# A second buffer for the output weights' pieces, and the mean of the last 256 tokens subtracted by adding DMAs

## The chip, the cores and the metric

The kernel runs on one core of a Trainium2 chip. The core has a matrix engine (TensorE, PE in the profile), a vector engine (VectorE, DVE), a scalar engine (ScalarE, ACT), a general engine (GpSimd, POOL) and SyncE (SP), which here only issues DMAs. They run side by side, each through its own list of instructions in order, and wait for each other by semaphores; DMAs run on 16 engines of their own. The metric is the time of one execution on the device in microseconds.

## The reference

One decoder layer over 1024 tokens of width 2048, all in float32:

```python
h = x @ w_in + b_in
q, k, v, g_attn, u_pool, g_pool = split(h)
a = banded_sink_attention(q, k, v, sinks, bias, valid) * silu(g_attn)   # 16 heads, window 128
b = multiscale_pool(u_pool, w_pool, pool_scale) * silu(g_pool)          # windows 2, 4, 8, 16
mix = concat([a, b]) @ w_out
ple = sigmoid(x @ w_gate_ple) * (p @ w_ple)
y = layer_norm(2 ** 0.25 * x + mix + ple, ln_gain, ln_bias)
```

The layer norm subtracts from every token the mean over its 2048 channels, divides by the standard deviation, and applies a gain and a bias for each channel.

## The kernel before

**Layout and precision.** Everything is kept with channels on the 128 partitions and tokens along the free axis. Every float32 operand is split into a high part (rounded, by ScalarE's cast) and a low part (the rest, by VectorE's subtraction), and each product is three matmuls: high by high, low by high, high by low (`mm3`, L181 to L185).

**Products.** A job multiplies two blocks of 128 output channels by half of the input channels for all 1024 tokens. Of the four quarter products of its 2 by 2 block form, seven combined ones are enough (a fast matrix product; their names are p1 to p7, their operands b11, b21, t1 and so on). One of these products is 12 matmuls of 128 x 512, about 2.7 us, and is called a tick: a counter of the program, `clock`, is raised by one after each, and all side work is booked by it. `after(n, fn)` records fn at the n-th tick from now; `later(n, fn)` does so as well, and puts what fn records behind the marked newest instructions of the engines. The final order on each engine is made by the scheduler of the language from that, with the data dependencies; the order of a queue is fixed before the run.

**Weights.** Weight pieces arrive in the tiles raw (512 KB each, five buffers), are split into wh (ScalarE, L816) and wl (VectorE, L126), four units ahead of TensorE.

**Stages.** s1 and s2: queries, keys, values and the other inputs, one half of the input channels after the other; s3: the rest with the per-layer embedding; s4 and s5: the output projection of the pooled and of the attended half; s6: the last 256 tokens of the output projection. Tokens 0 to 767 go through s5 with 384 columns a matmul, tokens 768 to 1023 through s6 (`run_plain`) with plain products of 256 columns.

**Attention beside s2.** For each pair of heads and quarter of the tokens, `heads` books by ticks: loads of the queries (s<-q) and of two bias masks (s<-in_rel), a split, score products (sc, L613), maxima on VectorE (L616), exponentials on ScalarE (L632), transposes (tr, L649), and value products (pv, L665). Their tiles are slots, of which 15 are handed round in turn.

**Centred output weights, beside s2.** `centre_weights` reads the attended half of w_out in 32 pieces of 256 KB through one tile, cw, sums their rows on VectorE (wsum, L950), and then reads all 32 again, subtracts the mean over the output channels (cw, L126) and stores them (wc). So the attended half of the projection has mean zero over the channels and needs no mean subtracted later. A piece is loaded at its tick and used two ticks later; the next is loaded at that same tick.

**The rest of the mean.** s4 leaves its sums (embedding, residual and pooled half) in DRAM (co, 16 blocks of 1024 tokens) and adds them up over the channel blocks in csum. `split_total` and `mean_to_subtract` turn csum into minus the mean of each token (L992). For tokens 0 to 767 it is taken away in s5: for four of the output blocks by adding csum on VectorE (d<-d,csum), for the others by one more matmul at the end of a product, with a constant matrix w64 and the split mean z (`less_mean`, L1007). For the last 256 tokens each of the 16 output blocks gets one such matmul in `run_plain` (L515). In s5 a finished block gets what lies in co added by a DMA of POOL (d<-co or part<-co, L436) and is squared for the norm six ticks later.

**The end.** `norm_scale` and `norm_out` scale tokens 0 to 767 while s6 runs; the last 256 tokens are scaled after it.

Of the kernel before, what the change touches and what calls it, by code (L numbers as in the profile page):

```python
# [24 lines left out]
F32 = mybir.dt.float32  # L25
F32R = mybir.dt.float32r
AF = mybir.ActivationFunctionType
ALU = mybir.AluOpType
# [3 lines left out]
P = 128  # L32
T = 512
H = 4 * P
D = 2048
NB = 16
# [14 lines left out]
F1, F2 = 768, 256  # L51
# [14 lines left out]
class Layer:  # L66
# [203 lines left out]
    def two(self):  # L270
        return self.tile(self.twos, [P, 2, self.F], "two")
# [227 lines left out]
    def run_plain(self, g):  # L499

        nc = self.nc
        (job,), order = self.groups[g]
        for i in range(2):
            ps = self.bank(BANKS[0][i], 2)[:, :F2]
            final = job.mean and i
            for u in range(2):
                wh, wl = self.take()
                for k in range(4):
                    f = slice(k * P, (k + 1) * P)
                    mm = self.mm3(ps, (wh[:, f], wl[:, f]), self.x_plain(4 * u + k), u + k == 0, False)  # L510
                if final and not u:
                    t = self.new_part(job.b[i])
                    nc.tensor.matmul(ps, self.ident, t, start=False, stop=False, skip_group_check=True)
                if u:
                    mm = self.less_mean(ps, F1)  # L515
                self.mark("PE", mm)
                self.feed_raw()
                if u and final:
                    job.done(job.b[i], ps)
                    nc.vector.tensor_copy(out=t, in_=ps)  # L520
                elif u:
                    t = self.new_part(job.b[i])
                    self.add_to(t, ps, False)
                    job.done(job.b[i], t)
                self.tick()
# [49 lines left out]
    def heads(self, h, j, half):  # L575

        nc, g = self.nc, j // 4
# [5 lines left out]
        two = lambda t: t.rearrange("p (j t) -> p j t", j=2)  # L583

        def begin():
            f = slice(h * T + 256 * half, h * T + 256 * half + 256)
            q = self.slot()[:, :T]
            rq.append(q)
            for i in range(2):
                self.load(two(q)[:, i], self.qd[j + i][:, f])  # L590
            for i in range(2):
                bias.append(self.slot()[:, :T].rearrange("p (e k) -> p e k", e=2))
                self.load(bias[i], self.rel[j + i])
# [82 lines left out]
                    self.load(self.pre[j + i][:, f], pre[0][:, i])  # L676

        begin()
        self.later(3, split)
        for n in range(2):  # L680
            for i in range(2):
                self.after(6 + 4 * n, lambda n=n, i=i: score(n, i))
            self.after(9 + 4 * n, lambda n=n: shift(n))
            self.after(15 + 4 * n, lambda n=n: trans(n))
            for i in range(2):
                self.after(10 + 4 * n, lambda n=n, i=i: softmax(n, i))
                self.later(12 + 4 * n, lambda n=n, i=i: share(n, i))
            self.after(21 + 4 * n, lambda n=n: value(n))


    def gate_ahead(self, j):
# [245 lines left out]
    def centre_weights(self, at, by):  # L937

        nc = self.nc
        cells = [(b, h) for b in range(NB) for h in range(2)]  # L940
        sums = self.fix.tile([P, 8, NB], F32, name="wsum")
        mean = self.fix.tile([P, 8], F32, name="wmean")
        now = []

        def fetch(b, h):
            now.append(self.load(self.tile(self.cw, [P, H], "cw"), self.wout[b, 0][:, h * H : h * H + H]))

        def add_up(b, h):
            k = now.pop().rearrange("p (k m) -> p k m", k=4)
            nc.vector.reduce_sum(sums[:, 4 * h : 4 * h + 4, b : b + 1], k, axis=mybir.AxisListType.X)  # L950

        def take_mean():
            nc.vector.reduce_sum(mean.rearrange("p (k b) -> p k b", b=1), sums, axis=mybir.AxisListType.X)
            nc.vector.tensor_scalar(out=mean, in0=mean, scalar1=1.0 / D, scalar2=None, op0=ALU.mult)

        def centre(b, h):
            w = now.pop()
            k = w.rearrange("p (k m) -> p k m", k=4)
            m = mean[:, 4 * h : 4 * h + 4].rearrange("p (k m) -> p k m", m=1).broadcast_to([P, 4, P])
            self.tt(k, k, m, ALU.subtract)  # L960
            self.load(self.wc[b, 0][:, h * H : h * H + H], w)

        for step in (add_up, centre):
            for c in cells:
                self.after(at, lambda c=c: fetch(*c))
                self.later(at + 2, lambda c=c, step=step: step(*c))
                at += by if step is centre and c[0] % 3 else 2
            if step is add_up:
                self.later(at + 1, take_mean)
                at += 2  # L970

    def split_total(self, total, w, cut):
# [9 lines left out]
    def mean_to_subtract(self, total, w):  # L982

        nc = self.nc
        h = F1 // 2
        for f, pieces in self.total_parts:
            ps = self.bank("sc", 2)
            for i, t in enumerate(pieces):  # L990
                nc.tensor.matmul(ps, w, t, start=i == 0, stop=i == 1)
            nc.scalar.activation(total[:, f], ps, AF.Copy, scale=-64.0 / D)  # L992
        step = self.one["new"]("q")[:, :h]
        self.tt(step, total[:, h:F1], total[:, :h], ALU.subtract)
        self.z, self.w64, self.total = {}, w, total
        a, b = slice(0, 64), slice(64, P)
        zs = [self.tile(self.twos, [P, 2, h], "two", F32R).rearrange("p h t -> p (h t)") for _ in range(2)]
        hi = self.one["new"]("hi")
        for at, src in ((0, total[:, :h]), (h, step), (F1, total[:, F1:])):
            n = src.shape[-1]  # L1000
            z = self.z[at] = zs[at // F1][:, at % F1 : at % F1 + n]
            nc.scalar.copy(out=hi[b, :n], in_=src[b])
            nc.scalar.copy(out=z[a], in_=src[a])
            self.tt(z[b], src[b], hi[b, :n].bitcast(F32), ALU.subtract)
# [18 lines left out]
    def norm_sums(self, sums, a, first, last):  # L1023

        for b in range(a.shape[-1] // P):
            self.nc.tensor.matmul(sums[:, b : b + 1], a[:, b * P : (b + 1) * P], self.ones[:, 0:1], start=first and b == 0, stop=last,
                                  skip_group_check=True)

    def norm_scale(self, L, wait=0):
# [55 lines left out]
    def run(self):  # L1085
        nc, tc, fix = self.nc, self.tc, self.fix
# [18 lines left out]
        co = [self.scratch("co") for _ in range(NB)]  # L1105
# [14 lines left out]
        ga, gp, u = ([(win, *p) for p in pairs(b, 4)] for b in (GA0, GP0, U0))  # L1120
# [63 lines left out]
        for o in reversed(BESIDE):  # L1184
            u = UNITS[o]
            operand[u] = ExitStack()
            self.xp[u] = self.pool(f"x_{u}", 1, operand[u], reuse_waits="tile")
        parts, work, over = ExitStack(), ExitStack(), ExitStack()
# [76 lines left out]
        self.turn.clear()  # L1265
        self.ident = fix.tile([P, P], F32, name="ident")
        make_identity(nc, self.ident)
        self.ones = fix.tile([P, P], F32, name="ones")
        nc.gpsimd.memset(self.ones, 1.0)
        self.mhalf = fix.tile([P, 8], F32, name="mhalf")  # L1270
        nc.gpsimd.memset(self.mhalf, -0.5)
# [10 lines left out]
        work = ExitStack()  # L1282
        self.new_part = lambda b: self.tile(pp, [P, 2, T], "part")
        self.slot_n = T
        self.slots = self.work_pool("slots0", 15, work)
        self.kv = self.work_pool("kv", 1, over)

        def build_kv(b, build, group, halves=(0, 1)):
# [5 lines left out]
        t = 9  # L1294
# [18 lines left out]
        for i in range(n3):  # L1313
            if i == 1:
                over.close()
                work.close()
                work, over = ExitStack(), ExitStack()
# [6 lines left out]
            if i == n3 - 2:  # L1324

                over.close()
                work.close()
                work = ExitStack()
                self.slot_n = T
                six[:] = 5 * [pp] + 3 * [self.work_pool("p8", 3, work)]  # L1330
                self.slots = self.work_pool("slots1", 8, work)
                self.twos = self.work_pool("twos1", 4, work)
                self.new_part = part_of_six
                for n, b in enumerate(s3[-4].b + s3[-3].b):
                    self.after((1, 1, 5, 6)[n], lambda b=b: self.gate_ahead(b - GA0))
                pooled()
                for n, step in enumerate(make_pooled):
                    self.after((10, 13, 16, 19, 22, 28, 31)[n], step)
                for n, b in enumerate(b for j in s3[-2:] for b in j.b):
                    self.after(16 + 2 * n, lambda b=b: self.gate_ahead(b - GA0))  # L1340
            first = self.groups[g + i][0][0]
# [8 lines left out]
        csum = []  # L1350
# [54 lines left out]
        w64 = self.tile(d0, [P, P], "w64", F32R, bufs=1)  # L1405
        self.later(9, lambda: self.split_total(csum[0], w64, [(0, T), (T, 2 * T)]))
        self.later(10, lambda: self.mean_to_subtract(csum[0], w64))
        self.new_part = new_d
        one = self.one = self.norm_begin(F1, 0, lambda kind: self.tile(lns, [P, F1], "sq" if kind == "sq" else "q", F32R if kind == "hi" else F32,
                                                                       bufs=1 if kind == "sq" else 2))  # L1410
# [119 lines left out]
```

## Time and profile before

Three runs took 1445.77, 1445.88 and 1448.65 us; the median is 1445.88. The profiled execution took 1448.33 us, of which the span from the first to the last instruction is 1446.6.

| Engine | busy us | share of the span | instructions |
|---|---|---|---|
| TensorE, matmuls | 1429.2 | 99% | 6820 |
| VectorE | 1115.5 | 77% | 2045 |
| ScalarE | 792.1 | 55% | 1565 |
| GpSimd | 232.8 | 16% | 339 |

The mean granted clock of TensorE was 0.996 of full speed. Matmuls overlap in the profile, so TensorE's busy time says that it is not idle, not that it runs at its peak; its gaps are in the list of waits. A line of a timeline has start, duration, engine, line, operation and tiles (written <- read), and in brackets the idle time of the engine before it and what ended it. SPq stands for SyncE's queue of DMA issues. A line of a list of waits has the total, the number of waits and the longest, all in us. The stages in time: s1 to about 180 us, s2 with the attention to about 700, s3 to 1108, s4 to 1260, s5 to 1383, s6 to 1430, then the last norm.

### The profile page before, as it was taken

The page shows a single profiled execution, that of the slowest core. Times are in us where ns is not written, and L with a number is a line of the kernel's source. Part 1 is how long each engine was busy: PE and PEld are TensorE (multiplying, and loading weights), DVE is VectorE, ACT ScalarE, POOL GpSimd, SP SyncE. Part 2 cuts the span into 40 slices and gives each one's busy share as a digit, 9 for nine tenths or more (in the row PEclk, how much of TensorE's full clock was granted, in tenths as well). Part 3 has the DMA queues.
Part 4 walks back from the last instruction along what each step waited for, and adds up shares of the span by engine and source line. Part 5 has one row for each costly group of instructions (what it writes and reads, how often), then busy time and mean ns, then how long its engine had stood idle before and what let it go on. Part 6 is the DMA issues. An engine that isn't in the chain of part 4 may idle for free.

```text
span 1446.6 us, 20400 instructions
## 1 busy us (share of the span) xinstructions
PE 1429.2 (99%) x6820; PEld 1210.5 (84%) x6820; DVE 1115.5 (77%) x2045; ACT 792.1 (55%) x1565; POOL 232.8 (16%) x339
## 2 busy tenths in 40 slices
PE   9999999999999999999999999999999999999996
PEld 7888887888888888888888888888888888899996
DVE  6859567787788877878768876867678665987787
ACT  6546375665667656665664444443356433654476
POOL 0000202211122211212111211211001211111223
PEclk9999999999999999999999999999999999999998
DMA  9463877455456655566887869998699768494566
GB/s 358 180 240 120 233 204 225 154 180 177 159 192 200 206 176 184 196 212 211 219 248 210 227 206 287 343 274 266 193 303 308 218 179 232 131 280 111 118 238 228
DMA packets 119226, 311.86 MB, mean 216 GB/s; under 512 B 13585, under 2 KB 27281, under 8 KB 119121
## 3 DMA queue, kind: packets, MB, share of 16 engines
q1 hardware_dynamic: 94480, 230.08, 46.5%
q0 software_dynamic: 21312, 73.15, 21.4%
q10 hardware_dynamic: 3328, 7.34, 1.5%
q8 instruction: 53, 0.87, 0.2%
q14 instruction: 53, 0.43, 0.1%
HBM read 211.95 MB, written 98.57 MB: 215 GB/s over the span
## 4 chain that ended last, share of the span: by engine, by line
PE 90%; DMA 4%; issue 2%; DVE 2%; ACT 1%; POOL 0%; POOLq 0%; SPq 0%; DVEq 0%; ACTq 0%
PE qa L183 15%; PE qa L185 15%; PE qa L184 15%; PE qb L185 11%; PE qb L183 11%; PE qb L184 11%; DMA part<-r 2%; PE sc L613 2%; PE pv L665 2%; DMA cw<-in_wout 2%; PE sc L185 1%; PE sc L183 1%; PE sc L184 1%; PE tr L649 1%; DVE wl L126 0%
## 5 line engine op out<-in xcount | busy, mean ns | idle before, releaser
L816 ACT CAST wh<-raw 128x512 fp32r<-128x512 f32 x428 | 264.3, 619 | 402.9 <-PE qa L184 156.6
L126 DVE TENSOR_TENSOR wl<-raw,wh 128x512 fp32r<-128x512 f32 x428 | 295.2, 693 | 105.2 <-ACT wh L816 100.3
L423 ACT COPY part<-qa 128x512 f32<-128x512 f32 (+1 forms) x180 | 104.0, 578 | 83.9 <-PE qa L185 81.5
L126 DVE TENSOR_TENSOR part<-part,qb 128x512 f32<-128x512 f32 (+1 forms) x120 | 81.1, 676 | 45.2 <-PE qb L185 40.6
L183 PE MATMUL qa<-b11h,wh 128*128 128x512 f32 (+2 forms) x292 | 108.9, 373 | 0.4 <-ACT part L423 0.4
L183 PE MATMUL qb<-b21h,wh 128*128 128x512 f32 (+2 forms) x292 | 108.9, 373 | 0.0
L185 PE MATMUL qa<-b11h,wl 128*128 128x512 f32 (+2 forms) x292 | 108.7, 372 | 0.0
L185 PE MATMUL qb<-b21h,wl 128*128 128x512 f32 (+2 forms) x292 | 108.7, 372 | 0.0
L184 PE MATMUL qa<-b11l,wh 128*128 128x512 f32 (+2 forms) x292 | 108.6, 372 | 0.0
L184 PE MATMUL qb<-b21l,wh 128*128 128x512 f32 (+2 forms) x292 | 108.5, 372 | 0.0
L183 PE MATMUL qa<-t3h,wh 128*128 128x512 f32 (+1 forms) x260 | 100.5, 387 | 2.2 <-ACT part L423 2.2
L184 PE MATMUL qa<-t3l,wh 128*128 128x512 f32 (+1 forms) x260 | 100.3, 386 | 0.0
L185 PE MATMUL qa<-t3h,wl 128*128 128x512 f32 (+1 forms) x260 | 100.3, 386 | 0.0
L183 PE MATMUL qa<-t2h,wh 128*128 128x512 f32 (+1 forms) x260 | 100.1, 385 | 0.1
L183 PE MATMUL qb<-t1h,wh 128*128 128x512 f32 (+1 forms) x260 | 99.9, 384 | 0.0
L185 PE MATMUL qa<-t2h,wl 128*128 128x512 f32 (+1 forms) x260 | 99.8, 384 | 0.0
L183 PE MATMUL qb<-b22h,wh 128*128 128x512 f32 (+1 forms) x260 | 99.7, 384 | 0.0
L185 PE MATMUL qb<-t1h,wl 128*128 128x512 f32 (+1 forms) x260 | 99.7, 384 | 0.0
L185 PE MATMUL qb<-b22h,wl 128*128 128x512 f32 (+1 forms) x260 | 99.7, 383 | 0.0
L185 PE MATMUL qa<-t4h,wl 128*128 128x512 f32 (+1 forms) x260 | 99.7, 383 | 0.0
L183 PE MATMUL qa<-t4h,wh 128*128 128x512 f32 (+1 forms) x260 | 99.6, 383 | 0.0
L184 PE MATMUL qb<-t1l,wh 128*128 128x512 f32 (+1 forms) x260 | 99.6, 383 | 0.0
(336 smaller groups left out, 3494.3 us busy)
## 6 DMA issues: line engine op xcount, KB each, us to landing
raw<-in_win SPq DMA_DIRECT2D x65, 512.0 KB, 4.2
h<-part SPq DMA_DIRECT2D x34, 512.0 KB, 3.0
part<-h POOLq DMA_DIRECT2D x34, 512.0 KB, 6.6
cw<-in_wout SPq DMA_DIRECT2D x64, 256.0 KB, 3.0
raw<-in_wgate SPq DMA_DIRECT2D x32, 512.0 KB, 4.9
raw<-wc SPq DMA_DIRECT2D x32, 512.0 KB, 4.4
s<-in_x SPq DMA_DIRECT2D x44, 256.0 KB, 5.7
s<-in_rel SPq DMA_DIRECT2D x32, 256.0 KB, 4.3
```

The source lines that it names most:

```text
L126: return (eng or self.nc.vector).tensor_tensor(out=out, in0=a, in1=b, op=op)
L183: mm(ps, wh, xh, start=start, stop=False, skip_group_check=True)
L184: mm(ps, wh, xl, start=False, stop=False, skip_group_check=True)
L185: return mm(ps, wl, xh, start=False, stop=stop, skip_group_check=True)
L423: self.mark("ACT", self.nc.scalar.copy(out=dst, in_=ps))
L613: nc.tensor.matmul(ps[:, e, z:], q, kk[:, keys], start=k == 0, stop=k == 1)
L649: nc.tensor.transpose(ps[:, o : o + P], sc[n, i][:, e, P:], self.ident)
L665: nc.tensor.matmul(ps, w, t, start=i == 0, stop=i == len(ms) - 1)
L816: ins = self.nc.scalar.copy(out=out, in_=a)
```

## The change

1. cw gets a second buffer, cw2; the two take turns. A piece is used three ticks after its load is booked, not two. The number of slots falls from 15 to 14.
2. In `heads` the loads of the bias masks are booked two ticks later, and the value products one tick earlier.
3. The last two of the seven splits of the pooled operands, at the end of s3, are booked with `later` in place of `after`, and at ticks 27 and 30 in place of 28 and 31.
4. The sixteen matmuls that took the mean from the last 256 tokens in `run_plain` are gone, with the splitting of that part of the mean in `mean_to_subtract`. In place of them, minus the mean of these tokens is added to co in DRAM: one adding DMA on POOL for each of the 16 blocks, 128 x 256 elements, booked at ticks 16 to 46 of s5. The sums that s6 reads from co then have the mean taken away.
5. The tile of ones keeps one column, the only one that was read.

The core of the diff:

```diff
--- before.py
+++ after.py
@@ run_plain
-                    mm = self.mm3(ps, (wh[:, f], wl[:, f]), self.x_plain(4 * u + k), u + k == 0, False)
+                    mm = self.mm3(ps, (wh[:, f], wl[:, f]), self.x_plain(4 * u + k), u + k == 0, u + k == 4)
                 if final and not u:
                     t = self.new_part(job.b[i])
                     nc.tensor.matmul(ps, self.ident, t, start=False, stop=False, skip_group_check=True)
-                if u:
-                    mm = self.less_mean(ps, F1)
@@ heads
             for i in range(2):
                 self.load(two(q)[:, i], self.qd[j + i][:, f])
+
+        def masks():
             for i in range(2):
                 bias.append(self.slot()[:, :T].rearrange("p (e k) -> p e k", e=2))
                 self.load(bias[i], self.rel[j + i])
...
         begin()
+        self.after(2, masks)
...
-            self.after(21 + 4 * n, lambda n=n: value(n))
+            self.after(20 + 4 * n, lambda n=n: value(n))
@@ centre_weights
-        now = []
+        now, cws = [], [self.cw, self.cw2]
 
         def fetch(b, h):
-            now.append(self.load(self.tile(self.cw, [P, H], "cw"), self.wout[b, 0][:, h * H : h * H + H]))
+            cws.append(cws.pop(0))
+            now.insert(0, self.load(self.tile(cws[0], [P, H], "cw"), self.wout[b, 0][:, h * H : h * H + H]))
...
                 self.after(at, lambda c=c: fetch(*c))
-                self.later(at + 2, lambda c=c, step=step: step(*c))
+                self.later(at + 3, lambda c=c, step=step: step(*c))
                 at += by if step is centre and c[0] % 3 else 2
             if step is add_up:
-                self.later(at + 1, take_mean)
+                self.later(at + 2, take_mean)
@@ mean_to_subtract
-        for at, src in ((0, total[:, :h]), (h, step), (F1, total[:, F1:])):
+        for at, src in ((0, total[:, :h]), (h, step)):
@@ run
-        self.slots = self.work_pool("slots0", 15, work)
+        self.slots = self.work_pool("slots0", 14, work)
+        self.cw2 = self.work_pool("cw2", 1, work)
...
-                    self.after((10, 13, 16, 19, 22, 28, 31)[n], step)
+                    (self.later if n > 4 else self.after)((10, 13, 16, 19, 22, 27, 30)[n], step)
...
         self.later(10, lambda: self.mean_to_subtract(csum[0], w64))
+        for b in range(NB):
+            self.after(16 + 2 * b, lambda b=b: nc.gpsimd.dma_start(out=co[b][:, F1:], in_=csum[0][:, F1:], accum_op=ALU.add))
```

How the order moves. The first place is SyncE's queue at the beginning of s2, some 30 issues into the row sums of the output weights. cw is a piece of these, raw a weight tile, s a slot, q and in_rel the queries and the masks. Before:

```order
L140 DMA q_151<-part_1783 128x1024
L140 DMA cw_2106<-in_wout 128x512
L140 DMA cw_2153<-in_wout 128x512
L140 DMA cw_2213<-in_wout 128x512
L140 DMA s_2309<-q_146 128x256
L140 DMA s_2309<-q_147 128x256
L140 DMA s_2312<-in_rel 128x512
L140 DMA s_2314<-in_rel 128x512
L140 DMA raw_2279<-in_win 128x1024
```

The same place with the change:

```order
L140 DMA cw_2104<-in_wout 128x512
L140 DMA raw_2102<-in_win 128x1024
L140 DMA q_150<-part_1781 128x1024
L140 DMA q_151<-part_1782 128x1024
L140 DMA s_2106<-in_rel 128x512
L140 DMA s_2108<-in_rel 128x512
L140 DMA cw_2155<-in_wout 128x512
L140 DMA cw_2215<-in_wout 128x512
L140 DMA s_2311<-q_146 128x256
L140 DMA s_2311<-q_147 128x256
L140 DMA cw_2284<-in_wout 128x512
L140 DMA raw_2282<-in_win 128x1024
```

One cw load has moved ahead of the weight tile and the q stores, the masks of the same head stand apart from its queries, and no three cw loads follow each other here.

The second place is GpSimd's queue in s5, from the last stores of co to the first adding DMAs of finished blocks. d and part are finished blocks, csum is minus the mean. Before:

```order
L145 DMA co_225<-part_11758 128x1024
L145 DMA co_226<-part_11759 128x1024
L145 DMA co_227<-part_11760 128x1024
L436 DMA d_12120<-co_216 128x768
L436 DMA d_12122<-co_218 128x768
L436 DMA d_12121<-co_217 128x768
L436 DMA d_12123<-co_219 128x768
```

With the change (L1412 is the line of the new DMAs):

```order
L1412 DMA co_213<-csum_11228 128x256
L1412 DMA co_214<-csum_11228 128x256
L1412 DMA co_215<-csum_11228 128x256
L1412 DMA co_216<-csum_11228 128x256
L436 DMA d_12124<-co_216 128x768
L1412 DMA co_217<-csum_11228 128x256
L436 DMA d_12126<-co_218 128x768
L1412 DMA co_218<-csum_11228 128x256
L1412 DMA co_219<-csum_11228 128x256
L436 DMA d_12125<-co_217 128x768
L1412 DMA co_220<-csum_11228 128x256
```

One more L1412 stands just ahead of this piece. So five of the new DMAs stand ahead of the first adding DMA of a finished block, six ahead of the second and eight ahead of the third.

More of the change, by code (lines that the diff above doesn't have):

```diff
@@ L996, in mean_to_subtract @@
         a, b = slice(0, 64), slice(64, P)
-        zs = [self.tile(self.twos, [P, 2, h], "two", F32R).rearrange("p h t -> p (h t)") for _ in range(2)]
+        zs = self.tile(self.twos, [P, 2, h], "two", F32R).rearrange("p h t -> p (h t)")
         hi = self.one["new"]("hi")
-        for at, src in ((0, total[:, :h]), (h, step), (F1, total[:, F1:])):
+        for at, src in ((0, total[:, :h]), (h, step)):
             n = src.shape[-1]
-            z = self.z[at] = zs[at // F1][:, at % F1 : at % F1 + n]
+            z = self.z[at] = zs[:, at : at + n]
             nc.scalar.copy(out=hi[b, :n], in_=src[b])
@@ L1025, in norm_sums @@
         for b in range(a.shape[-1] // P):
-            self.nc.tensor.matmul(sums[:, b : b + 1], a[:, b * P : (b + 1) * P], self.ones[:, 0:1], start=first and b == 0, stop=last,
+            self.nc.tensor.matmul(sums[:, b : b + 1], a[:, b * P : (b + 1) * P], self.ones, start=first and b == 0, stop=last,
                                   skip_group_check=True)
@@ L1267, in run @@
         make_identity(nc, self.ident)
-        self.ones = fix.tile([P, P], F32, name="ones")
+        self.ones = fix.tile([P, 1], F32, name="ones")
         nc.gpsimd.memset(self.ones, 1.0)
```

## The prediction

> **What bounds the kernel now.** I read the page first, then TensorE's list of waits, then the timelines around its longest waits. Of the page, the span, TensorE's busy time and the chain of waits:
>
> ```profile
> span 1446.6 us, 20400 instructions
> PE 1429.2 (99%) x6820; PEld 1210.5 (84%) x6820; DVE 1115.5 (77%) x2045; ACT 792.1 (55%) x1565; POOL 232.8 (16%) x339
> PE 90%; DMA 4%; issue 2%; DVE 2%; ACT 1%; POOL 0%; POOLq 0%; SPq 0%; DVEq 0%; ACTq 0%
> ```
>
> TensorE is at work for all but 17.4 us, so an edit can only pay by taking work off TensorE or by closing one of its few gaps. The list of its waits (total, times, longest) names the largest:
>
> ```profile
> PE qa L183 <- ACT part L423: 2.7, 2, 2.2
> PE sc L1054 <- POOL st L126: 1.1, 1, 1.1
> ```
>
> The second lies in the last normalisation, which the change leaves alone. The first is two gaps. The timelines of SP, DVE, ACT and PE around the longer one (start, duration, engine; in brackets the idle time before and what ended it):
>
> ```profile
> 216.82 13.72 SPq L140 DMA_DIRECT2D cw<-in_wout  x3
> ...
> 229.50 0.69 DVE L950 TENSOR_REDUCE wsum<-cw 128x4 f32<-128x512 f32 x1 [2.20 <-DMA cw<-in_wout]
> ...
> 233.43 0.21 ACT L625 ACTIVATE st<-st 128x4 f32<-128x4 f32 x1 [3.76 <-DVE st L126]
> ...
> 236.02 0.57 ACT L423 COPY part<-qa 128x512 f32<-128x512 f32 x1
> ...
> 236.65 0.67 PE L183 MATMUL qa<-t3h,wh 128*128 128x512 f32 x1 [2.25 <-ACT part L423]
> ```
>
> Read upwards, it explains itself: TensorE wanted bank qa, which ScalarE had not yet copied out; ScalarE stood behind an exponential that waited for VectorE's maxima; VectorE had stood still for 2.20 us at a row sum of the output weights, whose piece (cw) was still in flight, because the one cw buffer lets the next load go only after the last sum. The gap of 2.25 us is that 2.20 us. It has a second price, shown by the busy times of the stretches in and behind it (PEclk, the granted clock, is the third value from the end):
>
> ```profile
> 234.00:236.60 2.60, 0.40 (x2) 0.00 (x0) 2.38 (x8) 2.60 (x11) 1.45 (x2) 1.00 0.85 248
> 236.80:240.20 3.40, 3.40 (x9) 2.63 (x10) 0.65 (x2) 2.88 (x4) 0.00 (x0) 0.50 0.99 245
> ```
>
> For 3.4 us after the gap the clock is 0.50: half of 3.4 us, 1.7 us, is lost. [...]
>
> **The change part by part.**
>
> *A second cw buffer, used three ticks after its load.* A tick is one product. What SP waited for, from its own list of waits:
>
> ```profile
> SPq L140 <- DMA cw<-in_wout: 71.4, 31, 9.0
> SPq L140 <- DVE wsum L950: 36.1, 20, 8.1
> SPq L140 <- DVE cw L126: 28.3, 20, 4.5
> SPq L140 <- PE pv L665: 21.2, 8, 6.3
> ```
>
> The first three, 135.8 us of SP's queue, come from the one buffer: each load waits until the piece before has landed and been used. With two buffers a load needs the piece before last, which by the ticks is used one tick ahead of it. So the load goes out earlier, VectorE finds its piece there, and the 2.25 us gap goes. The cost in DMAs is nil: the same 64 loads and 32 stores. It is paid with one work slot (15 to 14); the mask loads two ticks later and the value products one tick earlier shorten what the slots hold. No instruction of the attention is added. These moves lie under TensorE's products; without that cover they cost what the gap cost.
>
> *The last two splits of the pooled operands, put behind the marks and at ticks 27 and 30.* ScalarE's and TensorE's timelines at the end of the stage:
>
> ```profile
> 1106.70 1.05 ACT L816 CAST b22h<-two 128x1024 fp32r<-128x1024 f32 x1 [2.62 <-DMA two<-cc]
> 1107.65 0.58 ACT L423 COPY part<-qa 128x512 f32<-128x512 f32 x1
> ...
> 1108.28 0.50 PE L183 MATMUL qa<-b11h,wh 128*128 128x512 f32 x1 [0.41 <-ACT part L423]
> ```
>
> A cast waits 2.62 us for its operand's load while TensorE's bank copy stands behind it. Moved behind the copy, the cast no longer holds it: 0.41 us gained. What is late next would be the product that reads b22, four ticks after tick 27, several us.
>
> *Sixteen mean products less.* TensorE's timeline in the last stage, the busy times there (after the sum: PE, PEld, DVE, ACT, POOL), and the tightest weight piece:
>
> ```profile
> 1389.67 0.28 PE L185 MATMUL qb<-b21h,wl 128*128 128x256 f32 x1
> 1389.79 0.28 PE L1007 MATMUL qb<-two,w 128*128 128x256 f32 x1
> 1389.90 0.28 PE L183 MATMUL qa<-b11h,wh 128*128 128x256 f32 x1
> ...
> 1400.00:1410.00 10.00, 10.00 (x88) 10.00 (x87) 9.96 (x18) 9.10 (x16) 4.87 (x9) 1.00 0.92 290
> 1410.00:1420.00 10.00, 10.00 (x88) 10.00 (x87) 10.00 (x19) 9.35 (x16) 5.01 (x11) 1.00 0.98 354
> ...
> 1420.79 1.29 DVE L126 TENSOR_TENSOR wl<-raw,wh 128x512 fp32r<-128x512 f32 x2
> ...
> 1422.35 0.28 PE L185 MATMUL qa<-b21h,wl 128*128 128x256 f32 x1
> ```
>
> The 0.28 us of one overlap; starts are 0.115 us apart, so sixteen are worth 1.84 us. VectorE has no idle time from 1400 on and writes the weights' low parts barely in time: the pair that begins at 1420.79 and is used at 1422.35 ends (1.29 us later, at 1422.08) 0.27 us before that, and its first half, the one used there, some 0.6 us earlier, 0.9 us of slack. TensorE, 14 products earlier at that point, would want it 1.6 us sooner. So the gain is between 0.9 and 1.84; I take 1.6, since VectorE too starts that stretch earlier. The splitting of the mean's third piece (two casts and a subtraction on half the partitions) falls away on ScalarE and VectorE; neither holds TensorE there: 0.
>
> *Sixteen adding DMAs on POOL.* No row of before shows one of this shape, or one that adds into DRAM. The nearest are the adding DMAs d<-co (384 KB, into SBUF): their group, the third of the first four, and the scaled sums that the new ones wait for; then the page's row of POOL's queue (packets, MB, share):
>
> ```profile
> L436 POOL DMA_DIRECT2D d<-co x6 | 5.3, 877 | 26.2 <-DVE d L126 21.4 <-issue 2.8 <-ACT d L423 2.0
> ...
> 1290.76 0.88 POOL L436 DMA_DIRECT2D d<-co  x1 [0.54 <-ACT d L423]
> ...
> 1283.62 0.60 ACT L992 ACTIVATE csum<-sc 128x512 f32<-128x512 f32 x1 [0.34 <-PE sc L991]
> ...
> q0 software_dynamic: 21312, 73.15, 21.4%
> ```
>
> In the new order eight of the sixteen, and two d<-co, stand on POOL ahead of that third d<-co. From 1284.2 (the sums are scaled), ten issues of 0.877 us end at 1293.0: it goes out 2.2 us later than at 1290.76. On the 16 DMA engines POOL's queue takes 21.4% of 1446.6 us for 73.15 MB, 4.2 us a MB: 0.55 us for 128 KB (131,072 bytes), 4.4 us for eight. The two do not add up, since the queue drains while the issue is late. VectorE, in order, waits for that d<-co; what hangs on it, with the DMA share (next to last value) of the two stretches:
>
> ```profile
> 1298.53 0.96 DVE L126 TENSOR_TENSOR d<-d,csum 128x768 f32<-128x768 f32 x1 [0.15 <-DMA d<-co]
> ...
> 1300.96 0.69 DVE L126 TENSOR_TENSOR wl<-raw,wh 128x512 fp32r<-128x512 f32 x1 [0.87 <-ACT wh L816]
> 1302.81 0.56 DVE L126 TENSOR_TENSOR part<-part,qa 128x384 f32<-128x384 f32 x1 [1.15 <-ACT q L1017]
> ...
> 1311.85 0.68 DVE L126 TENSOR_TENSOR wl<-raw,wh 128x512 fp32r<-128x512 f32 x1
> ...
> 1312.59 0.44 PE L185 MATMUL qa<-t2h,wl 128*128 128x384 f32 x1
> ...
> 1296.00:1300.00 4.00, 4.00 (x25) 4.00 (x24) 3.49 (x5) 1.62 (x3) 0.00 (x0) 1.00 1.06 245
> 1300.00:1304.00 4.00, 4.00 (x25) 4.00 (x24) 1.98 (x4) 2.98 (x5) 0.00 (x0) 1.00 0.53 184
> ```
>
> There is no slack at the d<-co (0.15 us waited already); 0.87 + 1.15 = 2.02 us of VectorE's idle time absorb a delay; and the low part written from 1311.85 to 1312.53 is used at 1312.59, 0.06 us of slack. So lateness costs TensorE what it has over 2.1 us. At most this d<-co is late by the whole 4.4 us, at a cost of 2.3; at least by nothing, if the eight fit into the 7.8 us that it takes to land already (1290.76 to 1298.53). The DMA engines are full until 1300, which is nearer to the upper end: I take three quarters, late by 3.3, cost 1.2 us. A gain is excluded, as nothing there gets earlier but two small operations. The d<-co that follow have the emptier stretch behind 1300; the loads that read what was added come only in the last stage.
>
> [...]
>
> **The sum.** The profiled execution took 1448.33 us (span 1446.6 and 1.73 around it). Against it: -2.25 -1.7 -0.41 -1.6 +1.2 = -4.76, 1443.6. The median of the runs shown, 1445.88, is 2.45 lower; the three lie at 1445.77, 1445.88 and 1448.65, two levels. One stretch of half clock is 1.7 of such a step, so I read the lower level as the gap without the half clock, and leave that term out: 1445.88 -2.25 -0.41 -1.6 +1.2 = **1442.8 us**, 0.21% faster.
>
> **Rivals.**
>
> *More is won.* Either the median holds the half clock too (1442.8 - 1.7 = 1441.1), or the adding DMAs are hidden (1441.6). For the first: the clock fell after this gap in the trace. Against: the two levels of the runs.
>
> *The adding DMAs take the place of the gap.* TensorE waits the full 2.3 us near 1312: 1442.8 + 1.1 = 1443.9; and as a gap of 2.25 us halved the clock once, this one may too: 1445.6. For it: DMA share 1.06. Against: absorbed idle time.
>
> *The gap is not won.* DMAs of that stretch are slow enough that three ticks do not suffice, or the faster runs never had it: 1442.8 + 2.25 = 1445.1. Against: SP held its loads 13.72 us for three pieces, which two buffers undo.
>
> *Slower: the mask loads hold SP.* With 14 slots a mask load waits for a slot that the value or transpose products of an earlier head must free, and the weight loads behind it on SP come late. Before, SP waited 21.2 us for such products, at most 6.3. One such stall that reaches TensorE costs what the old gap did, 2.25 + 1.7; it decides from two of them on: 1442.8 + 7.9 = 1450.7. Against it: SP was held 13.72 us in one place and no weights came late, only the piece that VectorE waited for.
>
> **How the numbers follow.** Forecast 0.37, more won 0.24, adding DMAs in place of the gap 0.22, gap not won 0.07, mask loads 0.10. What a measurement of this kernel can tell from no change is about 0.2%, 2.9 us: under 1443.0 is faster, over 1448.8 slower. The forecast's own spread (gain of 0.9 to 1.84, cost of 0 to 2.3) puts it under 1443.0 in some 0.24 of its 0.37; with the 0.24 of more won, faster is 0.48. Slower is the mask case, 0.10; the rest, 0.42, within. The range 1440.4 to 1446.5 leaves out the mask case and the last of the half-clock cases.
>
> **What would show it.** In the profile after: TensorE's wait for ACT part L423 gone or under 0.5 us, granted clock 1.00 from 200 to 260; SP's waits for cw under 40 us; no L1007-like product of 256 columns; DVE's idle time at its second d<-d,csum near 3 us (4.5 or more, with a gap of TensorE soon after, is the second rival). Wrong would be a new TensorE gap of over 2 us in the attention's stretch, or SP rows of s<-in_rel that wait longer than the cw rows did.

## The result, and the profile after

The changed kernel is slower: 1453.98 us (median of five runs, 1452.8 to 1456.69) beside 1445.88 (median of five). The ratio on record is 1.0044 with a 95% interval of 1.0026 to 1.0062; the quotient of the two medians is 1.0056. The forecast was 1442.8 us, faster, in a range from 1440.4 to 1446.5.

| | before | after |
|---|---|---|
| median, us | 1445.88 | 1453.98 |
| profiled execution, us | 1448.33 | 1452.95 |
| its span, us | 1446.6 | 1451.2 |
| TensorE busy, us | 1429.2 | 1427.8 |
| GpSimd busy, us | 232.8 | 251.0 |

TensorE's list of waits, after (total, times, longest):

```profile
PE qa L183 <- DVE part L126: 8.3, 1, 8.3
...
PE qa L183 <- ACT wh L817: 0.7, 1, 0.7
PE qa L183 <- ACT part L423: 0.3, 1, 0.3
```

The old gap (ACT part L423, 2.7 us in two waits) is down to 0.3. In its place stands one gap of 8.3 us, in the stage s5. Timelines of TensorE and VectorE around it, and the stretches from its beginning on (the third value from the end is the granted clock, the next the DMA share):

```profile
1307.72 0.69 PE L183 MATMUL qa<-t4h,wh 128*128 128x384 f32 x1 [8.30 <-DVE part L126]
...
1294.74 0.96 DVE L126 TENSOR_TENSOR d<-d,csum 128x768 f32<-128x768 f32 x1 [2.57 <-DMA d<-co]
1305.04 0.96 DVE L126 TENSOR_TENSOR d<-d,csum 128x768 f32<-128x768 f32 x1 [9.34 <-DMA d<-co]
...
1307.12 0.55 DVE L126 TENSOR_TENSOR part<-part,qa 128x384 f32<-128x384 f32 x1
...
1299.10:1303.10 4.00, 0.31 (x2) 0.00 (x0) 0.00 (x0) 0.00 (x0) 2.67 (x3) 1.00 0.61 82
1303.10:1307.70 4.60, 0.00 (x0) 0.00 (x0) 2.66 (x5) 1.35 (x2) 2.38 (x3) 0.50 0.85 127
1307.70:1313.30 5.60, 5.58 (x17) 5.58 (x18) 3.76 (x6) 1.92 (x3) 1.18 (x2) 0.50 0.97 213
```

TensorE wanted bank qa; VectorE had to empty it (part<-part,qa), but stood for 9.34 us at its second d<-d,csum, which waited for the third d<-co. That is the wait that the prediction named, with a price of 1.2 us. Behind the gap TensorE runs 5.6 us at half clock, 2.8 us lost. 8.3 + 2.8 + 0.7 (a smaller wait 10 us behind it, the second row of the list) = 11.8 us.

Why the third d<-co came late is read from GpSimd's timeline, after:

```profile
1279.31 2.72 POOL L1412 DMA_DIRECT2D co<-csum  x3 [6.63 <-ACT csum L994]
1286.67 0.88 POOL L1412 DMA_DIRECT2D co<-csum  x1 [4.64 <-issue]
1287.79 0.86 POOL L1412 DMA_DIRECT2D co<-csum  x1 [0.25 <-DMA two<-cc]
1288.92 0.88 POOL L436 DMA_DIRECT2D d<-co  x1 [0.26 <-issue]
1290.37 0.88 POOL L1412 DMA_DIRECT2D co<-csum  x1 [0.57 <-issue]
1291.44 0.89 POOL L436 DMA_DIRECT2D d<-co  x1 [0.19 <-issue]
1295.02 0.86 POOL L1412 DMA_DIRECT2D co<-csum  x1 [2.69 <-issue]
1297.12 0.89 POOL L1412 DMA_DIRECT2D co<-csum  x1 [1.24 <-issue]
1300.20 0.89 POOL L436 DMA_DIRECT2D d<-co  x1 [2.19 <-issue]
```

Three adding DMAs go out one behind the other, then GpSimd stands still, with nothing released that it waited for ("issue"). What it waits for shows when the DMA's own time is added. The first of the three takes 7.1 us to land (the view of its tile, least, median and most):

```profile
DMA to landing us min/median/max: 7.1/7.1/7.1
```

1279.31 + 7.05 (7.1 rounded) = 1286.36, and the fourth goes out at 1286.67, 0.31 us behind that. So it goes on: each of the next eight, of which the third d<-co is the last, goes out 0.3 us after the landing of the one three places ahead of it. Not the issue (0.88 us) but the landing (3.3 to 8.4 us here) of three at a time sets the pace, and the third d<-co goes out 20.9 us behind the first of them. (The profile puts the wait at 1287.79 down to another DMA, two<-cc; it too ends 0.31 us after the landing three places ahead.) Before the change the same thing could be read in one row, the one right behind the third d<-co that the prediction quoted:

```profile
1286.72 0.89 POOL L436 DMA_DIRECT2D d<-co  x1 [7.55 <-DVE d L126]
...
1294.45 0.87 POOL L436 DMA_DIRECT2D d<-co  x1 [2.80 <-issue]
```

The first of these rows took 7.42 us to land, at 1294.14; the fourth d<-co went out 0.31 us later.

### The profile page after: what moved, and what is told of

Read it like the earlier page. It is cut to its first block, busy times and chain, and to the rows that moved or that the text cites. A ratio compares the mean times of both kernels' runs of the same rounds, so it can differ in the third digit from the quotient of the medians.

```text
span 1451.2 us, 20372 instructions
## 1 busy us (share of the span) xinstructions
PE 1427.8 (98%) x6804; PEld 1210.0 (83%) x6804; DVE 1115.4 (77%) x2044; ACT 791.0 (55%) x1563; POOL 251.0 (17%) x355
## 3 DMA queue, kind: packets, MB, share of 16 engines
q0 software_dynamic: 23616, 75.25, 22.6%
## 4 chain that ended last, share of the span: by engine, by line
PE 94%; DVE 2%; DMA 2%; issue 1%; POOL 1%; ACT 0%; SPq 0%; POOLq 0%; DVEq 0%; ACTq 0%
PE qa L185 16%; PE qa L183 16%; PE qa L184 16%; PE qb L183 12%; PE qb L185 12%; PE qb L184 12%; PE sc L613 2%; PE pv L665 2%; PE sc L185 1%; PE sc L183 1%; PE sc L184 1%; PE tr L649 1%; DVE wl L126 1%; DMA two<-cc 1%; DMA d<-co 0%
## 5 line engine op out<-in xcount | busy, mean ns | idle before, releaser
L423 ACT COPY part<-qa 128x512 f32<-128x512 f32 (+1 forms) x180 | 103.8, 577 | 82.8 <-PE qa L185 81.0
L184 PE MATMUL qa<-t4l,wh 128*128 128x512 f32 (+1 forms) x260 | 100.3, 386 | 0.0
```

The source lines that it names most:

```text
L184: mm(ps, wh, xl, start=False, stop=False, skip_group_check=True)
L423: self.mark("ACT", self.nc.scalar.copy(out=dst, in_=ps))
```

## The experiments

Theory A: GpSimd's adding DMAs go out only three at a time, and this makes the third d<-co late. Theory B: the adding DMAs take the DMA engines' time. Theory C: the loss lies, in part, in the other edits. Ratios are to the kernel before, run beside.

### Without the adding DMAs

```diff
-        for b in range(NB):
-            self.after(16 + 2 * b, lambda b=b: nc.gpsimd.dma_start(out=co[b][:, F1:], in_=csum[0][:, F1:], accum_op=ALU.add))
...
+                if u:
+                    mm = self.less_mean(ps, F1)
...
```

The split of the mean's third piece in `mean_to_subtract` is back as well.

> The change without its fourth part: the mean of the last 256 tokens is again subtracted by the sixteen matmuls of the last stage, and no new DMA stands on POOL; the other parts (second cw buffer, masks and values, the two splits, the narrow tile of ones) stay. Theory A (the adding DMAs on POOL go out only three at a time, each 0.31 us after the landing of the one three before it, and so make the third d<-co late) and theory B (the adding DMAs take the DMA engines' time and so make the d<-co land late) both say: TensorE's wait for part L126 of 8.3 us near 1300 us is gone with the half clock behind it, and the time is 1445.88 - 2.25 (the gap at 234 us) = 1443.6 us, with 0.4 less if the 1107 us gap is won and 0.5 more if it is worse. Theory C (some of the loss comes from the other parts) says 1447 or more.

Measured: 1442.49 us, ratio 0.9976 (0.9967 to 0.9986). The gap is gone; VectorE's first and second d<-d,csum run one behind the other, where 9.34 us lay between them:

```profile
1294.74 2.02 DVE L126 TENSOR_TENSOR d<-d,csum 128x768 f32<-128x768 f32 x2
```

Theory C falls: the other parts win 3.5 us (2.0 to 4.8 by the interval), where 2.66 was forecast for them.

### The adding DMAs alone

The kernel before, with the diff's edits to `run_plain`, `mean_to_subtract` and the sixteen DMAs, nothing else.

> The kernel before with the fourth part of the change alone: sixteen adding DMAs in place of the sixteen matmuls; one cw buffer, 15 slots, the splits at their old ticks. Theories A and B: the gap at 234 us (2.25) is there as before, the gap near 1300 us is there too, 8 us with about 3 us of half clock, so the time is 1445.88 - 1.6 + 8 + 3 = 1455 us. Theory C: under 1448 us.

Measured: ratio 1.0062 (1.0044 to 1.0081), from five runs of 1451.71 to 1458.47 us. A sixth execution of this kernel took 8230.33 us; no trace here shows why, and the ratio leaves it out. TensorE's waits:

```profile
PE qa L183 <- DVE part L126: 7.8, 1, 7.8
PE qa L183 <- ACT part L423: 2.8, 4, 1.3
```

The new gap and the old ones, as theories A and B say. The adding DMAs carry the whole loss.

### More room for GpSimd's DMAs

```diff
-    nc = _bacc.Bacc("TRN2", target_bir_lowering=False, num_devices=1, dynamic_dma_scratch_size=1024)
+    nc = _bacc.Bacc("TRN2", target_bir_lowering=False, num_devices=1, dynamic_dma_scratch_size=1536)
```

> The changed kernel with one number altered: dynamic_dma_scratch_size, the room set apart for POOL's DMAs, 1536 in place of 1024. No work and no order changes. Theory A, if the three in flight come from this room: five adding DMAs in flight, the third d<-co goes out several us earlier than the 20.9 us behind the first adding DMA, TensorE's gap near 1300 us falls from 8.3 us to under 3 us, and the time to 1446 us or less. Theory B: the same bytes pass through the same engines, so the d<-co land as late as before, the gap stays near 8 us and the time within 1.5 us of 1453. If the three come from something else, theory A says no change either, and the count in flight stays three.

Measured: 1445.9 us, ratio 0.9997 (0.9987 to 1.0007), 6.8 us under the changed kernel (1.0044 less 0.9997, of 1445.9). GpSimd's timeline, TensorE's longest wait, and the stretch of the gap:

```profile
1279.47 4.49 POOL L1412 DMA_DIRECT2D co<-csum  x5 [5.87 <-ACT csum L994]
1286.40 0.88 POOL L436 DMA_DIRECT2D d<-co  x1 [2.44 <-DVE raw L126]
...
1292.97 0.88 POOL L436 DMA_DIRECT2D d<-co  x1 [1.10 <-issue]
...
PE qa L183 <- DVE part L126: 3.0, 1, 3.0
...
1299.20:1302.30 3.10, 0.33 (x2) 0.01 (x1) 2.41 (x4) 1.35 (x2) 2.09 (x3) 1.00 1.15 204
```

Five adding DMAs go out at once, not three; the third d<-co leaves 13.5 us behind the first adding DMA, not 20.9; the gap falls from 8.3 to 3.0 (under 3 was expected). The bytes are the same, so theory B as the main cause falls: in the changed kernel the DMA share in the gap's first 4 us was 0.61, here it is 1.15. The engines had room; the queue did not use it. What is left, 3.0 us, is a little over the most that the prediction allowed (2.3), and here the engines are full, so theory B may account for this rest; no run separates it. The half clock behind it costs another 1.7 us (3.4 us at a mean granted clock of 0.61, then 6.4 us at 0.94).

So dynamic_dma_scratch_size sets how many of the adding DMAs are in flight: three with 1024, five here, and the next run shows the same.

### Less room

The same number at 512.

> The changed kernel with dynamic_dma_scratch_size 512 in place of 1024; nothing else altered. With 1024 the adding DMAs went out three at a time, with 1536 five. Theory A as it now stands (one less than a quarter of the room in steps of 64 bytes: 1024 gives 4 - 1, 1536 gives 6 - 1) says one adding DMA in flight, each some 3.5 us with the 0.31 us to the next issue; ten stand ahead of the third d<-co or are it, so it goes out some 32 us behind the first, where it was 20.9 us, TensorE's gap grows from 8.3 us to about 20 us and the time to 1465 us or more. Theory B: fewer DMAs at a time share the same engines, the bytes are the same; no change, 1453 us within 2.

Measured: 1560.13 us from two runs, ratio 1.0784 (1.0748 to 1.082). GpSimd's timeline:

```profile
1339.19 0.91 POOL L1412 DMA_DIRECT2D co<-csum  x1 [5.31 <-ACT csum L994]
1346.61 0.89 POOL L1412 DMA_DIRECT2D co<-csum  x1 [6.50 <-issue]
...
1381.30 0.88 POOL L436 DMA_DIRECT2D d<-co  x1 [2.59 <-issue]
```

One at a time: each of the ten behind the first waits 2.5 to 6.5 us at "issue". The third d<-co, the last of these rows, goes out 42.1 us behind the first adding DMA, and TensorE's longest wait is 28.3 us. One, three, five for 512, 1024, 1536: the number follows the room, one for each 256 of it, less one. Theory A's formula comes to the same; its quarter and its steps of 64 bytes are one way to write it, and no run shows them apart. The time rises far more than expected, since the earlier stages send adding DMAs too (part<-r and others), which I had not counted: those into part stood 95.5 us at "issue", and the first of the new DMAs goes out at 1339.19, where the changed kernel has 1279.31.

### Smaller adding DMAs

```diff
-dma_start(out=co[b][:, F1:], in_=csum[0][:, F1:], accum_op=ALU.add)
+dma_start(out=co[b][:, F1 : F1 + 64], in_=csum[0][:, F1 : F1 + 64], accum_op=ALU.add)
```

> The changed kernel with the adding DMAs cut to 64 of their 256 columns, 32 KB in place of 128 KB (the mean of the other 192 tokens of this part is not subtracted). Count, order and queue are the same. Theory A: three are in flight as before, each lands in not much under the 3.1 us that the quickest of 128 KB took, so ten turns still take over 12 us; the third d<-co goes out at least 4 us later than in the kernel before and TensorE's gap near 1300 us is 3 to 7 us; 1446 to 1451 us. Theory B: the engines' time falls to a quarter, 1.1 us in place of 4.4 for the eight ahead of the third d<-co: the gap falls under 2 us, 1443 us.

Measured: 1448.42 us, ratio 1.0011 (0.9999 to 1.0023). GpSimd, then TensorE's wait:

```profile
1280.61 2.72 POOL L1412 DMA_DIRECT2D co<-csum  x3 [5.93 <-ACT csum L994]
1286.92 0.87 POOL L1412 DMA_DIRECT2D co<-csum  x1 [3.59 <-issue]
...
PE qa L183 <- DVE part L126: 3.4, 1, 3.4
```

With a quarter of the bytes still three, and a gap of 3.4 us, inside theory A's 3 to 7 and not under B's 2. Bytes count too: what stands three places behind the fourth and fifth, of 32 KB, went out 2.7 us after them, where it had been 3.7 us with 128 KB. So places come free sooner, and the gap is 4.9 us shorter.

### Half the rows

```diff
-dma_start(out=co[b][:, F1:], in_=csum[0][:, F1:], accum_op=ALU.add)
+dma_start(out=co[b][:64, F1:], in_=csum[0][:64, F1:], accum_op=ALU.add)
```

> The changed kernel with the adding DMAs on the first 64 of their 128 partitions only, 64 KB each (from the other 64 features of these tokens the mean is not subtracted). What does the limit count? If adding DMAs, whatever their size: three in flight, an x3 row and then a wait of some 4 us, the gap of TensorE near 1300 us 3 to 8 us and the time near that of the run with 64 columns, 0.1% above the kernel before. If it is room that goes by rows of the DMA (the run with 64 columns kept all 128 rows and stayed at three): one of 64 rows takes half the room, so the five ahead of the first d<-co and that d<-co itself go out at once, without a wait, the third d<-co goes out 3 us or more earlier than there, the gap is under 2 us and the time 1443 us, 0.2% below the kernel before.

Measured: 1444.82 us, ratio 0.9981 (0.9967 to 0.9996). GpSimd's timeline and TensorE's wait:

```profile
1279.46 4.31 POOL L1412 DMA_DIRECT2D co<-csum  x5 [5.93 <-ACT csum L994]
1282.25 2.47 POOL L436 DMA_DIRECT2D d<-co  x1
...
PE qa L183 <- DVE part L126: 1.8, 1, 1.8
```

The five and the d<-co behind them go out without a stop, six in flight, and ratio and gap are as the second reading had them. Cutting columns to a quarter left the limit at three, cutting rows to half moved it to six: how many were in flight went by rows here, not by bytes.

### The adding DMAs in fours, later

```diff
-        self.nc.gpsimd.dma_start(out=t, in_=job.first(job.b[i]), accum_op=ALU.add)
+        add = self.nc.gpsimd.dma_start(out=t, in_=job.first(job.b[i]), accum_op=ALU.add)
+        self.added(add.ins)
...
-        for b in range(NB):
-            self.after(16 + 2 * b, lambda b=b: nc.gpsimd.dma_start(out=co[b][:, F1:], in_=csum[0][:, F1:], accum_op=ALU.add))
+        queue, turns = list(range(NB)), [0, 0, 0, 0, 0, 4, 0, 4, 0, 4, 0, 4]
+
+        def added(ins):
+            for _ in range(turns.pop(0) if turns else 0):
+                b = queue.pop(0)
+                with self.tc.issue_after(ins):
+                    nc.gpsimd.dma_start(out=co[b][:, F1:], in_=csum[0][:, F1:], accum_op=ALU.add)
...
```

> The changed kernel with the sixteen adding DMAs put in fours behind the sixth, eighth, tenth and twelfth adding DMA of a finished block (in the stretches of some 11 us in which POOL's queue is idle, from 1318 us on), and none ahead of the first d<-co. Bytes and count are the same. Theory A: the third d<-co goes out as early as before the change, the gap near 1300 us is gone, each four takes about 5 us of an 11 us stretch and nothing waits for them; 1443.6 - 1.6 (the sixteen matmuls) = 1442.0 us. Theory B: the gap near 1300 us is gone too, but VectorE's waits at the later d<-co grow by 2 us for each four, TensorE's waits there reach 1 to 2 us each, and the time is 1445 us or more.

Measured: 1440.94 us, ratio 0.9962 (0.9947 to 0.9977), faster than both kernels. GpSimd's first d<-co and first four, and VectorE's sums:

```profile
1281.34 0.89 POOL L437 DMA_DIRECT2D d<-co  x1 [8.44 <-DVE d L127]
...
1285.37 0.88 POOL L437 DMA_DIRECT2D d<-co  x1 [1.13 <-ACT d L424]
...
1302.00 1.75 POOL L437 DMA_DIRECT2D part<-co  x2 [12.27 <-DVE part L127]
1303.12 1.55 POOL L1419 DMA_DIRECT2D co<-csum  x1
1307.46 0.88 POOL L1419 DMA_DIRECT2D co<-csum  x1 [2.78 <-issue]
1310.02 1.78 POOL L1419 DMA_DIRECT2D co<-csum  x2 [1.68 <-issue]
...
1292.02 1.82 DVE L127 TENSOR_TENSOR d<-d,csum 128x768 f32<-128x768 f32 x2
1297.84 1.82 DVE L127 TENSOR_TENSOR d<-d,csum 128x768 f32<-128x768 f32 x2
```

The limit of three is still there (the waits for "issue"), but nothing waits for those DMAs: the last of the sixteen went out at 1354.46, and GpSimd's first load of the sums for s6, at 1360.53, waited for TensorE. VectorE waits at no d<-co. So no cost shows. The gain is theory A's, 1.1 us more than it forecast.

### The larger room on other kernels

The kernel before, with 1536 (the tile of ones cut to one column to make the room), and the kernel with the fours, with 1536.

> The kernel before with dynamic_dma_scratch_size 1536 in place of 1024 (and the tile of ones cut to the one column that is read, which makes the room). Control for the run of the changed kernel with 1536. Theory A: before the change only the fourth d<-co waited for a place, 2.8 us, and TensorE lost nothing by it, so 1445.3 us within 1 us. If the larger room is worth something by itself (more stores in flight anywhere), the time falls by over 2 us, and the gain of the changed kernel with 1536 is not all the gap's.

Measured: 1447.4 us, ratio 1.0007 (0.9993 to 1.0021). That is over the 1445.3 expected, by more than the 1 us allowed, but the kernel before stood at 1446.6 itself beside it.

> The changed kernel with both: the sixteen adding DMAs in fours behind the sixth, eighth, tenth and twelfth adding DMA of a finished block, and dynamic_dma_scratch_size 1536. Theory A: with the fours TensorE waits for no d<-co any more, so the larger room has nothing left to give: 1440.9 us within 1 us.

Measured: 1441.46 us, ratio 0.9964 (0.9952 to 0.9976). The room by itself is worth nothing that these runs can tell; in the changed kernel, where the adding DMAs stand ahead of a needed one, it is worth 6.8 us.

### The other parts, one by one

The kernel before with the adding DMAs alone, in fours:

> The kernel before with the fourth part of the change alone, its sixteen adding DMAs put in fours behind the sixth, eighth, tenth and twelfth adding DMA of a finished block. If the sixteen matmuls are worth 1.6 us and the fours cost nothing: the kernel before less 1.6, a ratio of 0.9989, with TensorE's gap near 234 us (1.2 to 2.4 us so far) still there; the rest of what the spread changed kernel won (some 2.5 us) then belongs to the second cw buffer and the splits. If the other parts are worth nothing, this kernel is as fast as the spread changed one, a ratio of 0.9965.

The kernel with the fours, with `self.after` and ticks 28 and 31 for the last two splits:

> The changed kernel with the adding DMAs in fours, and the last two splits of the pooled operands as they were before the change (at ticks 28 and 31, ahead of the marks). If the prediction's term for them holds, TensorE's gap near 1107 us of 0.4 us is back and the time is 0.4 us above that of the same kernel with the splits moved. If instead moving them is what opens the gap of 0.9 to 1.1 us near 1116 us, that gap is gone and the time 0.5 us or more below. If both gaps are there, moving them is worth 0.4 and the gap near 1116 us has another cause.

And the kernel with the fours again, beside these two:

> The spread changed kernel once more, on the chip and beside the runs of the two others: 0.9965 of the kernel before.

Measured: 0.9990 (0.9979 to 1.0), 0.9968 (0.9955 to 0.998) and 0.9965 (0.9952 to 0.9978). So by the ratios the matmuls are worth 1.4 us of 1445 (0 to 3.0 by the interval), the rest of the change 3.6, and the moved splits too little to be told (0.0003 in the ratio, 0.4 us, inside the intervals). The traces tell the matmuls' worth better: from the first product of 256 columns to the last, s6 took 50.04 us before (1382.76 to 1432.80) and 48.47 in the first of these three (1380.86 to 1429.33); over all profiles it is 1.3 to 1.7 us less without them. The share of the second cw buffer, with the moved masks and value products, from which no run separates it, is plain in the stretch from 180 to 700 us (TensorE's busy time is the second value), of the kernel before, of the first of these three (both with one buffer) and of the third (two buffers):

```profile
180.00:700.00 520.00, 517.41 (x2454) 430.40 (x2453) 423.93 (x1007) 332.71 (x824) 97.16 (x123) 1.00 0.59 193
180.00:700.00 520.00, 517.37 (x2459) 430.19 (x2458) 424.46 (x1010) 333.25 (x826) 95.65 (x123) 1.00 0.59 194
180.00:700.00 520.00, 519.66 (x2473) 432.50 (x2472) 427.20 (x1015) 335.63 (x829) 96.94 (x123) 1.00 0.59 194
```

2.6 us of TensorE's idle time there with one buffer, 0.3 with two: 2.3 us. The splits, in TensorE's timeline of the second of the three, with the old ticks:

```profile
1103.62 0.50 PE L184 MATMUL qa<-b11h,wh 128*128 128x512 f32 x1 [0.34 <-ACT part L424]
1116.04 0.47 PE L184 MATMUL qb<-t1h,wh 128*128 128x512 f32 x1 [1.25 <-ACT wh L819]
```

The 0.4 us gap is back with the old ticks, as the prediction's term has it: it stands in four of the five profiles with the old ticks (all but that of the kernel before with 1536) and in none with the new. The gap near 1116 us comes with both (0.93 after the change, 1.25 here) and is missing with both (in the third's profile, and in the kernel before). No run tells its cause; the moved splits are not it.

## Why the prediction was wrong

*The second cw buffer: right, the size in part by luck.* -2.25 was forecast, 2.3 us of TensorE's idle time in the stage is gone. But the forecast put it all on the one gap near 235 us. In the other three profiles with one buffer that gap is 1.0 to 1.4 us, and gaps near 486 and 651 us make up the rest (2.2 to 2.7 in all). The half clock behind it stands in the profile of the kernel before (a mean clock of 0.66 from 236 to 241 us), not in the two with the adding DMAs alone, ahead or in fours (1.00). The count of SP's waits was off: the three cw rows fall from 135.8 to 98.6 us (61.0 + 35.3, and 2.3 for the pieces to land), not under 40; what mattered was whose wait ends last, and VectorE's row sums, which had waited 8.9 us for cw, wait for it no more.

```profile
SPq L140 <- DVE wsum L952: 61.0, 20, 7.8
...
SPq L140 <- DVE cw L126: 35.3, 24, 4.8
```

*The two splits: the mechanism right, the size not measurable.* 0.41 forecast, the gap comes and goes with the edit, and a gap of about 1 us some 10 us later, in some executions, hides it.

*Sixteen mean products less: right.* 1.6 forecast; 1.3 to 1.7 in the traces. The times agree, with wide intervals: 1.4 by the ratio of the kernel before with the fours, 1.55 between the medians of the kernel without adding DMAs and the one with them in fours (1442.49 - 1440.94).

*The adding DMAs: wrong, and with them the sign.* The place was right (third d<-co, VectorE's second sum, TensorE behind it), the size was not: +1.2 forecast, 11.6 measured (1.0044 less 0.9964, the middle of the two results in fours, of 1445.9; the trace gave 11.8, the kernel before with the adding DMAs alone, less the same in fours, 10.4, and the medians 13.0). The step that failed is "ten issues of 0.877 us end at 1293.0: it goes out 2.2 us later". It took GpSimd's queue for one that only issues. Beside the kernel with the fours, which runs in step with the changed one up to there, the third d<-co goes out 14.8 us later (1300.20 for 1285.37) and the second sum begins some 12 us later. The two costs of the prediction, issues (2.2 us) and DMA engines (4.4), are both less than these 14.8; yet the larger was taken as the most. The row that shows it, a fourth d<-co that waits 2.80 us for "issue" until the first of three in flight had landed, stood right behind the row that I quoted, and the quoted group of six d<-co carries it as "<-issue 2.8". Two smaller errors were in the same term. The engines' time of an adding DMA is not 0.55 us:

```profile
q0 software_dynamic: 23616, 75.25, 22.6%
```

22.6% of 1451.2 less 21.4% of 1446.6 is 18.4 us for sixteen, 1.15 us each, twice the estimate from the queue's mean; other pairs of pages, with and without these DMAs, give 0.8 to 1.3. And what absorbs lateness was underestimated: some 12 us late made a gap of 8.3, so 3.7 us were absorbed, not 2.1; the wait came out at bank qa and not at the low part of the weights, which I had taken as the tightest.

*The rivals.* "The adding DMAs take the place of the gap", half clock behind it included, was the right story with a price capped at 2.3 us; its sign, 4.5 us or more of idle time of VectorE at the second d<-d,csum, came with 9.34. The mask loads did not hold SP: its waits for the value products fell from 21.2 to 15.5 us. The bet on two levels of the runs, with and without half clock, is not borne out either: 23 runs of the kernel before, beside the first experiments, fill the stretch from 1443.2 to 1449.7 us.

*The sum again, with measured terms:* -3.5 (the parts without the adding DMAs) - 1.5 (the matmuls) + 11.8 (the trace's price of the adding DMAs) = +6.8 us; the ratio 1.0044 is 6.4.

## What to carry to other kernels

GpSimd's queue of DMAs had three prices here: the issue, the engines' time (0.8 to 1.3 us for 128 KB), and how many may be in flight. The third makes the pace landing time over places: 3.3 to 8.4 us over three, 2.1 us for each of the ten on average, against 0.88 for the issue. Before work is put into a queue ahead of something that an engine waits for, look there for rows that wait for "issue", and count how many are still flying at that moment. And put such work behind the last DMA that is needed soon: the same sixteen DMAs cost 11.6 us ahead of it, and in fours behind it nothing that the runs can tell.

## What the runs showed of the hardware that was not expected

- Of GpSimd's adding DMAs with 128 rows, one, three or five are in flight with dynamic_dma_scratch_size 512, 1024 or 1536; the next goes out 0.3 us after a landing. With 1024, quarter columns kept three in flight, and half the rows let six out (five of 64 rows and one of 128).
- Of GpSimd's plain DMAs with 128 rows more were in flight. In the changed kernel's last loads of co, GpSimd issues fourteen (one stands ahead of these rows) all but without a stop; at most seven are in flight, and the first stop of over 0.2 us comes when seven are:

```profile
1372.62 3.22 POOL L145 DMA_DIRECT2D t1h<-co  x6
1375.83 2.66 POOL L145 DMA_DIRECT2D t1l<-co  x5
1378.47 1.08 POOL L145 DMA_DIRECT2D t2h<-co  x2
...
1381.52 0.54 POOL L145 DMA_DIRECT2D t2h<-co  x1 [1.24 <-issue]
```

- An adding DMA of 128 KB into DRAM cost the engines 0.8 to 1.3 us (by the shares of GpSimd's queue on pages with and without sixteen of them), where the queue's mean per byte gave 0.55.
- The clock fell to half 3.7 us into the gap of 8.3 us and stayed there for 10.2 us, until 5.6 us after TensorE had begun again; behind the gap of 2.25 us before the change it was 3.4 us. Behind a gap of 3.0 us (1536) it was 3.4 us (a mean of 0.66 from 1303 to 1308 us), with one of 3.4 (quarter columns) 6.8 (0.98 from 1299 to 1303 us, 0.50 to 1308, 0.83 to 1313). With gaps of up to 1.8 us (half the rows) there was none: the run's mean clock is 0.997, as with the fours.
